# The opening of a diffusion block: modulation weights re-laid, and two steps handed to GpSimd

## The chip, the cores and the metric

One core of one Trainium2 chip. The time is device microseconds from a timed execution of the whole kernel; lower is better. TensorE (PE) multiplies matrices, VectorE (DVE) and ScalarE (ACT) work element by element, GpSimd (POOL) does so too on its own queue, SyncE (SP) issues the DMAs. Each of them works through its own queue in order.

## The reference

One layer of a hybrid backbone in float32: a half-step SwiGLU FFN, token mixing (an mLSTM beside a spatial gating MLP), a second FFN, a final norm. There are 1024 latent tokens (`x`) and 256 context tokens (`ctx`), 1024 channels, and an FFN width of 2816. What matters here is how the layer starts:

```python
mods   = split(silu(c) @ w_ada + b_ada, 9)              # nine vectors of 1024, for the latent tokens
mods_c = split(silu(c_ctx)[None] @ w_ada + b_ada, 9)    # the same for the context

def ffn_sublayer(h, shift, scale, gate, g, w_in, w_out):
    hn = rmsnorm(h, g) * (1 + scale) + shift
    a, b = split(hn @ w_in, 2)
    return h + 0.5 * gate * ((silu(a) * b) @ w_out)

h  = ffn_sublayer(x + pos_emb, mods[0],   mods[1],   mods[2],   g_ffn1, w_ffn1_in, w_ffn1_out)
hc = ffn_sublayer(ctx,         mods_c[0], mods_c[1], mods_c[2], g_ffn1, w_ffn1_in, w_ffn1_out)
...                                                     # mixing, second FFN, final norm
```

`w_ada` is 1024 x 9216, that is nine parts of 1024 columns. Its first two parts give the shift and the scale of the first FFN, and no product of that FFN can begin without them.

## The kernel before, in words

Everything is held with channels on the 128 partitions, so a tensor of 1024 channels is eight blocks `d`. Large products run in three passes: each operand is split into a rounded part and a remainder (`hi`, `lo`), and for each block the passes are hi x hi, hi x lo and lo x hi (`mm3`, L182). `split` (L145, L146) makes the two parts of a weight: ACT copies the rounded one, VectorE subtracts for the remainder.

The kernel opens with the context's first FFN product (`pa`, `pb`, 22 steps `f`), since the context is small. `W` (class `Weights`) brings its weights: `load` issues the DMA of a raw weight of 128x1024 (L126) and splits it into `hl`; up to three are held.

Ahead of the first product stand four strands of work:

- *Norm of the context* (`nct`, class `Norm`). `sq` squares a block on ACT and adds it to `acc` on the engine given to the constructor (L209, seven adds of 128x256). `rstd` sums `acc` over the partitions on PE (L214), takes the inverse root on VectorE (L758 to L770), and writes it on two diagonals (`diag`, L224, L225). `bcast` spreads it over the partitions on PE (`rb`, L230). `scaled0` multiplies the eight blocks of the context by it on VectorE (L938).
- *Shift and scale* from the first two parts of `w_ada`, cut into four column quarters `qt` and four row groups `kp`, sixteen pages of 512 KB. Each page holds for two row blocks 256 columns of part 0 and 256 of part 1. Quarters 0, 1 and 3 are multiplied on PE (`ada_rows`, L850), copied on ACT (`ada_copy`), turned on PE (`ada_flip`, L859), and finished on VectorE (`ada_done`, L879 and L887). Quarter 2 is multiplied on VectorE instead: `side(kp, ...)` does four multiply-adds of 128x512 a page (L791, L793), then `ada_red` transposes and reduces (L797, L798), and `ada_side` finishes it (L867, L871).
- *The modulated context*: `mod0(d, d+1)` makes two blocks on ACT (L931 and L932: scale and shift, rounded copy) and their remainders (L934), the even block's on POOL and the odd one's on VectorE.
- *The first weights* (`W.load`).

In this opening the order on PE, VectorE and ACT is the order in which the program writes its steps (`manual_schedule`), up to the end of the first step `f == 0`; POOL's and SyncE's are set by a scheduler. Filling matmuls (`idle`, L922, products of constants into a bank that nobody reads) keep PE at work in between. The products of step 0 start with six of the eight blocks for `pa`; `last0` (quarter 3's `ada_flip`, `ada_done`, then `mod0(6, 7)` and the third weight) is put between `pa` and `pb`.

The pages of `w_ada` are read from the tensor as it is, 8 x 128 x 9216, by `ada_page` in two DMAs each. The other seven parts are read much later by `ada_load` (L782), in pieces of 128x512, for the gates and the later sublayers.

Of the kernel before, what the change touches and what calls it, by code (L numbers as in the profile page):

```python
# [9 lines left out]
F32 = mybir.dt.float32  # L10
# [3 lines left out]
ALU = mybir.AluOpType  # L14
# [9 lines left out]
NKT = D // 128  # L24
# [31 lines left out]
def _build(ctx, tc, nc, a, out):  # L56
    V, S, G, T = nc.vector, nc.scalar, nc.gpsimd, nc.tensor
# [5 lines left out]
    hnp = pool("hn")  # L63
# [37 lines left out]
    def mm_ps(name):  # L101
        return ps.tile([128, 512], F32, name=name, tag="mm", bufs=4)
# [4 lines left out]
    class Weights:  # L107
# [7 lines left out]
            self.held = 0  # L115
            self.n = 0

        def load(self):
            n, i, w = self.order.popleft()
            src = a[n][i]  # L120
            if self.n % 4 < 2:
                raw = self.pool.tile([128, w], F32, name="raw", tag="raw", bufs=2)
            else:
                raw = hnp.tile([128, w], F32, name="raw", tag="pg0" if self.n == 2 else "pg1", bufs=8)
            self.n += 1
            nc.sync.dma_start(raw, src)  # L126
            hl = self.pool.tile([128, 2, w], F32R, name="hl", tag="hl", bufs=3)
            split(hl, raw)
            self.ready.append((n, i, hl))
            self.held += 1  # L130

# [9 lines left out]
            while self.order and self.held < 3:  # L141
                self.load()

    def split(hl, src):
        hi = S.copy(hl[:, 0, :], src)  # L145
        return hi, V.tensor_sub(hl[:, 1, :], src, hl[:, 0, :].bitcast(F32))  # L146

    def behind(fn, ins):

# [628 lines left out]

    def ada_load(page, m, hf, k):
        pgt = page()  # L780
        o = m * 1024 + hf * 512
        nc.sync.dma_start(pgt, a["w_ada"][k, :, o:o + 512])  # L782
        return pgt

# [51 lines left out]
    QW = 1024 // NQ  # L836
    QD = QW // 128
    KP = 512 // QW

    def ada_page(qt, kp, tag):  # L840
        pg = hnp.tile([128, KP, 2, QW], F32, name="adapg", tag=tag, bufs=8)
        for i in range(KP):
            src = a["w_ada"][kp * KP + i].rearrange("p (m c) -> p m c", m=9)[:, 0:2, qt * QW:(qt + 1) * QW]
            nc.sync.dma_start(pg[:, i], src)
        return [pg[:, i].rearrange("p m c -> p (m c)") for i in range(KP)]

    def ada_rows(pr, pgs, kp):
        for i, pg in enumerate(pgs):
            k = kp * KP + i
            T.matmul(pr[0:2, 0:2 * QW], sc2[:, :, k], pg, start=k == 0, stop=k == NKT - 1, skip_group_check=True)  # L850

    def ada_copy(pr):
        row = t2("adrow", shape=(2, 2 * QW))
        S.copy(row, pr[0:2, 0:2 * QW])
        return row
# [42 lines left out]
    W = Weights([("w1i", f, 1024) for f in range(2 * NF)], "w1")  # L898
    A = Stage("1", "w1i", 3)
    h = A.h  # L900
    hcp = [fxpage("hc", F32, (128, 4, 256)) for _ in range(2)]
    hc = [hcp[d // 4][:, d % 4, :] for d in range(NKT)]
# [17 lines left out]
    def idle(n):  # L920
        for _ in range(n):
            T.matmul(junk[:, 0:128], ones, ones, start=True, stop=True)  # L922

    hncp = [fxpage("hnc", F32R, (128, 2, 2, 256)) for _ in range(4)]
    hnc = [hncp[d // 2][:, d % 2] for d in range(NKT)]
    nct = Norm(hc, 256, V)

    def mod0(*ds):
        ts = [t2("nt")[:, 0:256] for _ in ds]
# [6 lines left out]
    def scaled0():  # L936
        for d in range(NKT):
            V.tensor_tensor(hc[d], hc[d], nct.rb, ALU.mult)  # L938
# [5 lines left out]
    def side(kp, pgs):  # L944
        for i, pg in enumerate(pgs):
            for q in range(2):
                ada_acc(V, sides[q], pg, q, kp * KP + i, kp + i == 0)

    load_c(hcp, 4)
    pgs = {}  # L950
    for qt, kp in ((2, 0), (0, 0), (0, 1), (2, 1), (0, 2), (0, 3), (2, 2), (1, 0), (1, 1), (2, 3), (1, 2), (1, 3),
                   (3, 0), (3, 1), (3, 2), (3, 3)):
        pgs[qt, kp] = ada_page(qt, kp, "pg1" if qt % 2 else "pg0")
    idle(30)
    for d in range(NKT):
        nct.sq(d)
    side(0, pgs[2, 0])
    prs = {0: mm_ps("adr")}
    ada_rows(prs[0], pgs[0, 0], 0)
    nct.rstd()  # L960
    ada_rows(prs[0], pgs[0, 1], 1)
    idle(3)
    side(1, pgs[2, 1])
    ada_rows(prs[0], pgs[0, 2], 2)
    nct.bcast()
    ada_rows(prs[0], pgs[0, 3], 3)
    row = ada_copy(prs[0])
    scaled0()
    side(2, pgs[2, 2])
    idle(4)  # L970
    pc = sm_ps("adc")
    ada_flip(pc, row)
    ada_done(0, pc)
    mod0(0, 1)
    prs[1] = mm_ps("adr")
    for kp in range(NKT // KP):
        ada_rows(prs[1], pgs[1, kp], kp)
    row = ada_copy(prs[1])
    side(3, pgs[2, 3])
    reds = [cp.tile([128, 32], F32, name="adred", tag="adred", bufs=2) for _ in range(2)]  # L980
    for acc, red in zip(sides, reds):
# [4 lines left out]
    ada_flip(pc, row)  # L986
    ada_done(1, pc)
    mod0(2, 3)
    ada_rows(prs[3], pgs[3, 1], 1)
    ada_side(2, reds)  # L990
    for kp in (2, 3):
        ada_rows(prs[3], pgs[3, kp], kp)
    W.load()
    mod0(4, 5)
    row = ada_copy(prs[3])
    W.load()
# [157 lines left out]
    hc = [hcp[d // 2][:, d % 2, :] for d in range(NKT)]  # L1154
# [4 lines left out]
    for f in range(NF):  # L1159
        hl, g = wready.popleft()  # L1160
# [14 lines left out]
    nct = Norm(hc, 256, V)  # L1175
# [951 lines left out]
    m = [fxpage("m", F32, (128, 1024)) for _ in range(NKT)]  # L2127
# [101 lines left out]
def layout(x, c, ctx, c_ctx, w_ada, b_ada, g_ffn1, w_ffn1_in, w_ffn1_out, g_mix, w_in, b_gates,  # L2229
           conv_qk_w, conv_qk_b, g_head, g_sgu, w_s, b_s, w_branch_a, w_branch_b, w_out,  # L2230
           g_ffn2, w_ffn2_in, w_ffn2_out, g_final):
    f = np.float32

    def A(v):
        return np.asarray(v)
    x, c, ctx, c_ctx = A(x)[0], A(c)[0], A(ctx)[0], A(c_ctx)
    win = A(w_in)[0]
    off = {}
    o = 0
    for n, w in (("q", 1024), ("k", 1024), ("v", 1024), ("g", 16), ("o", 1024), ("u", 1024), ("vs", 1024), ("ga", 1024), ("gb", 1024)):  # L2240
        off[n] = win[:, o:o + w]
        o += w
    r = {}
    r["xT"] = np.ascontiguousarray(x.T).reshape(8, 128, 1024)
    r["cT"] = np.ascontiguousarray(ctx.T).reshape(8, 128, 256)
    parts = {
        "b_ada": _cols(A(b_ada)[0]), "g_ffn1": _cols(A(g_ffn1)[0]), "g_mix": _cols(A(g_mix)[0]),
        "g_ffn2": _cols(A(g_ffn2)[0]), "g_final": _cols(A(g_final)), "g_head": _cols(A(g_head)[0]),
        "g_sgu": _cols(A(g_sgu)[0]), "c": _cols(c), "c_ctx": _cols(c_ctx),
        "conv_w": np.concatenate([_cols(A(conv_qk_w)[0, j]) for j in range(3)], axis=1),  # L2250
        "conv_b": _cols(A(conv_qk_b)[0]),
    }
    r["vec"] = np.ascontiguousarray(np.concatenate([parts[n] for n in VEC], axis=1))
    s = np.arange(128)
    cst = np.zeros((128, 5, 128), f)
    cst[s, 0, s] = 1.0
    cst[:, 1, :] = (s[:, None] % 32 == s[None, :] % 32)
    cst[s, 2, 127 - s] = 1.0
    cst[:, 3, :] = np.where(s[:, None] <= s[None, :], 0.0, -BIG)
    cst[:, 4, :] = np.where(s[:, None] >= s[None, :], 0.0, -BIG)  # L2260
    r["cst"] = cst.reshape(128, 640)
    quarter = D // 4
    freqs = np.exp(f(-np.log(10000.0)) * np.arange(quarter, dtype=f) / f(quarter)).astype(f)
    rr = np.arange(16, dtype=f)[:, None] * freqs
    cc = np.arange(64, dtype=f)[:, None] * freqs
    rt = np.concatenate([np.sin(rr), np.cos(rr)], axis=1).astype(f)
    ct = np.concatenate([np.sin(cc), np.cos(cc)], axis=1).astype(f)
    rt = rt.T.reshape(4, 128, 16).transpose(1, 0, 2).reshape(128, 64)
    ct = ct.T.reshape(4, 128, 64).transpose(1, 0, 2).reshape(128, 256)
    r["pos"] = np.ascontiguousarray(np.concatenate([rt, ct], axis=1))  # L2270
    r["b_gates"] = np.ascontiguousarray(A(b_gates)[0]).reshape(1, 16)
    r["b_s"] = np.ascontiguousarray(A(b_s)[0]).reshape(1, 512)
    r["wsT"] = np.ascontiguousarray(A(w_s)[0].transpose(2, 0, 1)).reshape(128, 512)
    r["w_ada"] = np.ascontiguousarray(A(w_ada)[0]).reshape(8, 128, 9216)
    for n, w in (("w1i", w_ffn1_in), ("w2i", w_ffn2_in)):
        t = _tiles(A(w)[0])
        r[n] = np.ascontiguousarray(np.stack([t[:NF], t[NF:]], axis=1)).reshape(2 * NF, 128, 1024)
    r["w1o"] = np.ascontiguousarray(A(w_ffn1_out)[0]).reshape(NF, 128, 1024)
    r["w2o"] = np.ascontiguousarray(A(w_ffn2_out)[0]).reshape(NF, 128, 1024)
    for n, k in (("wq", "q"), ("wk", "k"), ("wo", "o"), ("wu", "u"), ("wga", "ga"), ("wgb", "gb")):  # L2280
        r[n] = _tiles(off[k])
    for n, k in (("wv", "v"), ("wvs", "vs")):
        r[n] = np.ascontiguousarray(off[k]).reshape(8, 128, 1024)
    r["wg"] = np.ascontiguousarray(off["g"].reshape(8, 128, 16).transpose(1, 0, 2)).reshape(128, 128)
    r["w_a"] = _tiles(A(w_branch_a)[0])
    r["w_b"] = _tiles(A(w_branch_b)[0])
    r["w_o"] = _tiles(A(w_out)[0])
    return r
# [18 lines left out]
```

## Time and profile before

| | |
|---|---|
| median of 3 runs | 2649.54 us (2647.95 to 2652.47) |
| span of the profiled execution, first to last instruction | 2647.6 us |
| its own time as a run | not listed apart; the fastest run is 2647.95 us, the median 1.94 us above the span |
| TensorE matmul / weight load | 2632.7 us (99%) / 2213.3 us (84%) |
| VectorE, ScalarE, GpSimd | 1947.2 us (74%), 1202.8 us (45%), 74.2 us (3%) |
| HBM read, written | 329.11 MB, 121.32 MB, 170 GB/s over the span |

The profile shows one execution. Busy times of engines overlap. In a timeline row stand the start in us, the length in us, the engine, the line of the program, the operation, output and inputs by the program's names, and a count; an idle time ahead of the row, with what ended it, is in brackets. In the chain of waits a row is a start, a length and what the end of the kernel was waiting for then. In a row by windows stand the window and its length, the busy time of PE, PE's weight loads, VectorE, ACT and POOL, each with a count of instructions, and at the end the granted TensorE clock, the busy share of the DMA engines, and GB/s.

### The profile page before, as it was taken

Reading aid. Unit: us, or ns where it says so; the run is one execution under the profiler, and the core shown is the slowest. Engines: PE = TensorE matmul, PEld = TensorE weight load, DVE = VectorE, ACT = ScalarE, POOL = GpSimd, SP = SyncE. Lnnn points to the kernel's source line nnn. Section 1 sums busy time; section 2 is a strip of 40 time slices with the busy share of each in tenths; the row PEclk is TensorE's granted clock in tenths of the full one; section 3 lists DMA queues with packets and bytes.
Section 4 is the critical chain, followed back from the end, with each engine's and each line's share of the span. In section 5 each row is a group of like instructions: output and inputs, shape, how many; then the busy total and the mean of one; then the engine's idle time right before and its main releaser. Section 6 shows DMA issues by size and latency. Waiting matters only on the chain.

```text
span 2647.6 us, 35932 instructions
## 1 busy us (share of the span) xinstructions
PE 2632.7 (99%) x12904; PEld 2213.3 (84%) x12904; DVE 1947.2 (74%) x3490; ACT 1202.8 (45%) x2167; POOL 74.2 (3%) x158
## 2 busy tenths in 40 slices
PE   9999999999999999999999999999999999999998
PEld 6998888888889878888888888888888888888887
DVE  7988688687989646787664878777568766665855
ACT  5664444444347525564443454333256444344433
POOL 0000000000000000000000002221000000000000
PEclk9999999999999999999999999999999999999999
DMA  9833344368587122356552466547341333337654
GB/s 314 308 111 136 119 163 167 112 233 309 172 278 263 65 80 91 104 184 197 188 178 105 151 218 243 175 154 267 131 142 41 127 140 115 120 123 277 200 160 178
DMA packets 201234, 452.73 MB, mean 171 GB/s; under 512 B 20320, under 2 KB 54624, under 8 KB 201056
## 3 DMA queue, kind: packets, MB, share of 16 engines
q1 hardware_dynamic: 200624, 450.05, 49.9%
q8 instruction: 101, 1.65, 0.3%
q14 instruction: 77, 0.63, 0.1%
q10 hardware_dynamic: 432, 0.39, 0.0%
HBM read 329.11 MB, written 121.32 MB: 170 GB/s over the span
## 4 chain that ended last, share of the span: by engine, by line
PE 94%; issue 2%; DMA 2%; DVE 1%; ACT 1%; POOL 0%; SPq 0%; POOLq 0%; DVEq 0%; ACTq 0%
PE qa L411 18%; PE pq L1377 17%; PE po L535 14%; PE qb L411 14%; PE pt L1856 10%; PE pr L1296 5%; PE pa L182 2%; PE pc L1165 2%; PE pb L182 2%; PE pn L2011 2%; PE pu L1697 1%; PE pn L2009 1%; PE pkc L1356 1%; PE pvc L1453 1%; PE sp L1975 1%
## 5 line engine op out<-in xcount | busy, mean ns | idle before, releaser
L146 DVE TENSOR_TENSOR ring<-rawq,ring 128x512 fp32r<-128x512 f32 x408 | 281.0, 690 | 225.5 <-ACT ring L145 224.2
L535 PE MATMUL po<-gring,wring 128*128 128x512 f32 (+1 forms) x1896 | 423.5, 384 | 0.0
L535 PEld LDWEIGHTS po<-gring,wring 128*128 128x128 f32 x1896 | 349.6, 188 | 69.9
L145 ACT CAST ring<-rawq 128x512 fp32r<-128x512 f32 x408 | 253.4, 622 | 312.3 <-PE pq L1377 87.0
L411 PE MATMUL qa<-fc,ring 128*128 128x512 f32 x1056 | 252.4, 389 | 0.0
L411 PEld LDWEIGHTS qa<-fc,ring 128*128 128x128 f32 x1056 | 198.2, 188 | 41.5 <-DVE fc L146 0.4
L1377 PE MATMUL pq<-fc,ring 128*128 128x512 f32 x864 | 208.5, 394 | 0.0
L145 ACT CAST wring<-rw 128x512 fp32r<-128x512 f32 x154 | 95.8, 623 | 217.2 <-PE po L535 183.0
L1377 PEld LDWEIGHTS pq<-fc,ring 128*128 128x128 f32 x864 | 162.2, 189 | 33.4
L1856 PE MATMUL pt<-yp,ring 128*128 128x512 f32 x768 | 184.8, 394 | 0.0
L1856 PEld LDWEIGHTS pt<-yp,ring 128*128 128x128 f32 x768 | 143.1, 188 | 28.2
L146 DVE TENSOR_TENSOR wring<-rw,wring 128x512 fp32r<-128x512 f32 x154 | 105.6, 686 | 81.4 <-ACT wring L145 81.0
L1377 PE MATMUL pq<-fa,ring 128*128 128x512 f32 x576 | 142.4, 395 | 0.0
L1377 PE MATMUL pq<-fb,ring 128*128 128x512 f32 x576 | 138.5, 394 | 0.0
L1377 PEld LDWEIGHTS pq<-fb,ring 128*128 128x128 f32 x576 | 107.7, 188 | 23.8 <-issue 0.2
L411 PE MATMUL qa<-fa,ring 128*128 128x512 f32 x528 | 127.0, 390 | 0.0
L411 PE MATMUL qa<-fb,ring 128*128 128x512 f32 x528 | 126.5, 390 | 0.0
L411 PE MATMUL qb<-fb,ring 128*128 128x512 f32 x528 | 126.5, 389 | 0.0
L411 PE MATMUL qb<-fc,ring 128*128 128x512 f32 x528 | 126.3, 389 | 0.0
L411 PE MATMUL qb<-fa,ring 128*128 128x512 f32 x528 | 126.2, 389 | 0.0
L1377 PEld LDWEIGHTS pq<-fa,ring 128*128 128x128 f32 x576 | 106.9, 188 | 22.3 <-DVE ring L146 0.2
L793 DVE SCALAR_TENSOR_TENSOR adacc<-adapg,sc,adacc 128x512 f32<-128x512 f32 x154 | 111.7, 745 | 15.7 <-DMA adapg<-in_w_ada_dram 14.7
(366 smaller groups left out, 4643.6 us busy)
## 6 DMA issues: line engine op xcount, KB each, us to landing
adapg<-in_w_ada_dram SPq DMA_DIRECT2D x144, 256.0 KB, 3.6
fsp<-fhl SPq DMA_DIRECT2D x66, 512.0 KB, 2.7
gring<-fsp SPq DMA_DIRECT2D x66, 512.0 KB, 4.1
raw<-in_w1i_dram SPq DMA_DIRECT2D x44, 512.0 KB, 5.3
graw<-fsp SPq DMA_DIRECT2D x88, 256.0 KB, 3.6
rawq<-in_w1i_dram SPq DMA_DIRECT2D x38, 512.0 KB, 3.7
rawq<-in_w2i_dram SPq DMA_DIRECT2D x38, 512.0 KB, 3.6
fsp<-p SPq DMA_DIRECT2D x66, 256.0 KB, 2.2
```

The costliest lines, as they stand in the source:

```text
L145: hi = S.copy(hl[:, 0, :], src)
L146: return hi, V.tensor_sub(hl[:, 1, :], src, hl[:, 0, :].bitcast(F32))
L182: T.matmul(pt, x, y, start=first and i == 0, stop=i == n - 1, skip_group_check=True)
L411: T.matmul(pt, hl[:, x, sl], pages[p][k][:, y, :], start=first and i == 0, stop=i == 11, skip_group_check=not first)
L535: T.matmul(pt[:, cs], w[:, x, sl], g[:, y, cs], start=grp and kp == 0 and i == 0, stop=kp == NFP - 1 and i == 2, skip_group_check=not grp)
L793: eng.scalar_tensor_tensor(acc, pgt, sc2[:, q, k:k + 1], acc, ALU.mult, ALU.add)
L1165: T.matmul(pt, hl[d // 4][:, x, sl], g[:, y, :], start=f == 0 and d % 2 == 0 and i == 0, stop=f == NF - 1 and i == 2, skip_group_check=True)
L1296: T.matmul(self.pt[m], pg[:, x, sl], hl[:, y, :], start=first and k == 0 and i == 0, stop=k == 3 and i == 2, skip_group_check=not first)
L1356: T.matmul(self.cp[:, o:o + 256], hl[:, x, k * 128:(k + 1) * 128], hnc[kc][:, y, :], start=p == 1 and k == 0 and i == 0, stop=p in (2, 4) ...
L1377: T.matmul(pt, hl[:, x, k * 128:(k + 1) * 128], pg[k][:, y, :], start=first and k == 0 and i == 0, stop=k == 3 and i == 2, skip_group_chec ...
L1856: T.matmul(pt, hl[:, x, k * 128:(k + 1) * 128], pg[:, y, :], start=kh + k + i == 0, stop=kh == 1 and k == 3 and i == 2)
L2011: T.matmul(pn[:, 0:257], qi[:, c_, :], self.C[d][:, c_, :], start=False, stop=c_ == 1)
```

## The change

The first two parts of `w_ada` become a tensor of their own, `w_ada0`, in sixteen blocks of 128 x 1024: one page is now one contiguous block, read in one DMA with 4 KB per partition instead of two with runs of 1 KB. The rest, `w_ada`, keeps seven parts, so `ada_load` counts its columns from part 2. The pages are loaded in another order. The adds of the context's squares go from VectorE to POOL, and so does the subtraction that makes the remainder of the first weight. Of the filling matmuls 26 of the first 30 stay, and the 3 and 4 that stood later are taken out. The written order of the opening changes: quarter 0's second page comes ahead of the row sums of `rstd`; its third and fourth and quarter 1's first page come ahead of `bcast`; `side(2, ...)` moves from before quarter 0's turn to before `side(3, ...)`; two more pages of quarter 3 come ahead of `ada_side`.

```diff
-        def load(self):
+        def load(self, eng=V):
...
-            split(hl, raw)
+            split(hl, raw, eng)
...
-    def split(hl, src):
+    def split(hl, src, eng=V):
         hi = S.copy(hl[:, 0, :], src)
-        return hi, V.tensor_sub(hl[:, 1, :], src, hl[:, 0, :].bitcast(F32))
+        return hi, eng.tensor_tensor(hl[:, 1, :], src, hl[:, 0, :].bitcast(F32), ALU.subtract)
...
-        o = m * 1024 + hf * 512
+        o = (m - 2) * 1024 + hf * 512
...
     def ada_page(qt, kp, tag):
-        pg = hnp.tile([128, KP, 2, QW], F32, name="adapg", tag=tag, bufs=8)
-        for i in range(KP):
-            src = a["w_ada"][kp * KP + i].rearrange("p (m c) -> p m c", m=9)[:, 0:2, qt * QW:(qt + 1) * QW]
-            nc.sync.dma_start(pg[:, i], src)
-        return [pg[:, i].rearrange("p m c -> p (m c)") for i in range(KP)]
+        pg = hnp.tile([128, KP, 2 * QW], F32, name="adapg", tag=tag, bufs=8)
+        nc.sync.dma_start(pg.rearrange("p k c -> p (k c)"), a["w_ada0"][qt * (NKT // KP) + kp])
+        return [pg[:, i] for i in range(KP)]
...
-    nct = Norm(hc, 256, V)
+    nct = Norm(hc, 256, G)
...
-    for qt, kp in ((2, 0), (0, 0), (0, 1), (2, 1), (0, 2), (0, 3), (2, 2), (1, 0), (1, 1), (2, 3), (1, 2), (1, 3),
+    for qt, kp in ((0, 0), (0, 1), (2, 0), (0, 2), (0, 3), (2, 1), (1, 0), (1, 1), (2, 2), (1, 2), (1, 3), (2, 3),
                    (3, 0), (3, 1), (3, 2), (3, 3)):
         pgs[qt, kp] = ada_page(qt, kp, "pg1" if qt % 2 else "pg0")
-    idle(30)
+    idle(26)
     for d in range(NKT):
         nct.sq(d)
-    side(0, pgs[2, 0])
     prs = {0: mm_ps("adr")}
     ada_rows(prs[0], pgs[0, 0], 0)
+    side(0, pgs[2, 0])
+    ada_rows(prs[0], pgs[0, 1], 1)
     nct.rstd()
-    ada_rows(prs[0], pgs[0, 1], 1)
-    idle(3)
-    side(1, pgs[2, 1])
     ada_rows(prs[0], pgs[0, 2], 2)
-    nct.bcast()
     ada_rows(prs[0], pgs[0, 3], 3)
     row = ada_copy(prs[0])
+    prs[1] = mm_ps("adr")
+    ada_rows(prs[1], pgs[1, 0], 0)
+    nct.bcast()
+    side(1, pgs[2, 1])
     scaled0()
-    side(2, pgs[2, 2])
-    idle(4)
     pc = sm_ps("adc")
     ada_flip(pc, row)
     ada_done(0, pc)
     mod0(0, 1)
-    prs[1] = mm_ps("adr")
-    for kp in range(NKT // KP):
+    for kp in (1, 2, 3):
         ada_rows(prs[1], pgs[1, kp], kp)
     row = ada_copy(prs[1])
+    side(2, pgs[2, 2])
     side(3, pgs[2, 3])
...
     mod0(2, 3)
-    ada_rows(prs[3], pgs[3, 1], 1)
+    for kp in (1, 2):
+        ada_rows(prs[3], pgs[3, kp], kp)
     ada_side(2, reds)
-    for kp in (2, 3):
-        ada_rows(prs[3], pgs[3, kp], kp)
-    W.load()
+    ada_rows(prs[3], pgs[3, 3], 3)
+    W.load(G)
     mod0(4, 5)
     row = ada_copy(prs[3])
     W.load()
...
-    r["w_ada"] = np.ascontiguousarray(A(w_ada)[0]).reshape(8, 128, 9216)
+    wada = A(w_ada)[0].reshape(8, 128, 9, 1024)
+    r["w_ada"] = np.ascontiguousarray(wada[:, :, 2:]).reshape(8, 128, 7168)
+    r["w_ada0"] = np.ascontiguousarray(wada[:, :, :2].reshape(4, 2, 128, 2, 4, 256).transpose(4, 0, 2, 1, 3, 5)).reshape(16, 128, 1024)
```

## The prediction, made before the changed kernel was run

> **What bounds the kernel now.** I read the page first, then the span cut in windows, then the chain and the engines' timelines over the first 46 us, where every edit but one lies.
>
> ```profile
> span 2647.6 us, 35932 instructions
> PE 94%; issue 2%; DMA 2%; DVE 1%; ACT 1%; POOL 0%; SPq 0%; POOLq 0%; DVEq 0%; ACTq 0%
> ```
>
> The chain that ended last is 94% TensorE. The windows (busy time by engine; the last columns are granted clock, DMA share, GB/s) show where it is not:
>
> ```profile
> 0.00:37.20 37.20, 35.85 (x151) 17.29 (x151) 25.34 (x71) 14.78 (x33) 2.86 (x9) 1.00 0.99 326
> 100.00:2647.00 2547.00, 2534.30 (x12240) 2134.02 (x12240) 1869.85 (x3351) 1149.45 (x2082) 70.05 (x148) 1.00 0.49 165
> ```
>
> Behind 100 us TensorE is busy 2534.30 of 2547 us, so the body can give back 12.7 us at most, and the change touches nothing there but the address of the `w_ada` loads. In the first 37.2 us PE looks busy too, but with filling matmuls and the small `adr` products; the first large product (`pa`) starts behind them. The chain of waits, in order of time (start, length, what), tells what it waits for:
>
> ```profile
> 1.64 4.22 DMA hc<-in_cT_dram
> 5.88 0.42 ACT acc L205
> ...
> 10.16 0.87 DVE adacc L791 x2
> ...
> 26.16 2.73 DVE adacc L793 x4
> ...
> 35.91 1.24 DVE hl L146
> 37.14 0.04 issue
> 37.19 2.18 PE pa L182 x16
> ```
>
> Nearly every piece between 6.6 and 37.1 us is VectorE. So I price the change as a shift of the moment at which `pa` has its weight's remainder, 37.19 us; what comes later moves with it, since PE is full from there on. VectorE's own timeline (start, length, line, operation), which the sum is made on:
>
> ```profile
> 6.63 3.60 DVE L209 TENSOR_TENSOR acc<-acc,sq 128x256 f32<-128x256 f32 x7 [5.44 <-ACT sq L208]
> 10.16 0.87 DVE L791 TENSOR_SCALAR adacc<-adapg,sc 128x512 f32<-128x512 f32 x2
> 10.95 1.41 DVE L793 SCALAR_TENSOR_TENSOR adacc<-adapg,sc,adacc 128x512 f32<-128x512 f32 x2
> 12.27 0.15 DVE L758 TENSOR_SCALAR rs_x<-p 128x2 f32<-128x2 f32 x1
> 14.86 0.64 DVE L225 SCALAR_TENSOR_TENSOR diag<-cst,rs_y,diag 128x128 fp32r<-128x128 f32 x2 [0.47 <-ACT diag L224]
> 15.42 2.73 DVE L793 SCALAR_TENSOR_TENSOR adacc<-adapg,sc,adacc 128x512 f32<-128x512 f32 x4
> 18.07 2.73 DVE L938 TENSOR_TENSOR hc<-hc,rb 128x256 f32<-128x256 f32 x8
> 20.72 2.73 DVE L793 SCALAR_TENSOR_TENSOR adacc<-adapg,sc,adacc 128x512 f32<-128x512 f32 x4
> 30.89 0.69 DVE L798 TENSOR_REDUCE adred<-adtr 128x16 f32<-128x512 f32 x1
> 35.91 1.23 DVE L146 TENSOR_TENSOR hl<-raw,hl 128x1024 fp32r<-128x1024 f32 x1
> 37.13 0.88 DVE L934 TENSOR_TENSOR hnc<-nt,hnc 128x256 fp32r<-128x256 f32 x1
> ```
>
> **The loads.** Thirty-two DMAs of 256 KB in runs of 1 KB become sixteen of 512 KB in runs of 4 KB, in another order: `(0,0) (0,1) (2,0) ...` where `(2,0)` was first. SyncE has half the issues, which pays nothing, since it was waiting for landings anyway. Rates, from two windows, one with `w_ada` pages, one with `w1i` weights in runs of 4 KB:
>
> ```profile
> 28.00:29.00 1.00, 1.00 (x3) 0.17 (x2) 1.00 (x3) 0.51 (x1) 0.00 (x0) 1.00 1.10 348
> 33.00:34.00 1.00, 1.00 (x3) 0.17 (x2) 0.12 (x1) 0.97 (x3) 0.72 (x1) 1.00 1.08 408
> 9.73 1.88 PE L850 MATMUL adr<-adapg,sc 128*2 128x512 f32 x4
> ```
>
> At 348 GB/s a page of 524 KB takes 1.51 us, at 408 GB/s 1.28 us. The second page was there at 9.73 us (third row: its products begin), so the pages' stream starts at 9.73 - 2 x 1.51 = 6.7 us, and the new third page, `(2,0)`, lands at 6.7 + 3 x 1.28 = 10.6 us; `side(0)` on VectorE waits for it, where it began at 10.16 us before. All sixteen are in by 27.2 us instead of 30.8 us, but their readers are VectorE's chain, so that gain lies beside it. If the rate stays at 348, the page lands at 11.2 us.
>
> **Squares on POOL.** Seven adds (3.60 us) leave VectorE, but the same row-sums are still needed by `rstd`. POOL's prices (two rows with min/median/max in ns, two of its timeline), and PE's for the sums:
>
> ```profile
> L2185 POOL TENSOR_TENSOR h<-h,rbs x6: 726/730/740, 2633.5 to 2643.0; 128x256 f32<-128x256 f32 x6
> L2005 POOL TENSOR_TENSOR qi<-qT,ib x128: 447/459/958, 1583.5 to 1819.2; 128x128 f32<-128x128 f32 x128
> 32.99 0.73 POOL L934 TENSOR_TENSOR hnc<-nt,hnc 128x256 fp32r<-128x256 f32 x1 [7.34 <-ACT hnc L932]
> 36.23 1.49 POOL L934 TENSOR_TENSOR hnc<-nt,hnc 128x256 fp32r<-128x256 f32 x1 [2.52 <-ACT hnc L932]
> 11.54 0.60 PE L214 MATMUL p<-ones,acc 128*128 128x1 f32 x4
> ```
>
> An add of 128x256 is 0.73 us, so the sum, begun at 6.65 us as before, is done at 6.65 + 7 x 0.73 = 11.8 us, against 10.2 us. The 36.23 row is the warning: the same operation took 1.49 us while VectorE's `hl` subtraction (35.91 to 37.14) ran, and VectorE's next one, at 37.13, took 0.88 us, where a 128x256 one costs about 0.5 (3.60 / 7). The two engines hold each other up. `side(0)` (2.19 us from 10.16 to 12.35) now falls on the last adds: by 10.6 us POOL has done 5.4, and 1.6 x 0.73 = 1.15 us are left. One behind the other, both are done at 10.6 + 2.19 + 1.15 = 13.95 us; if nothing is held up, VectorE is free at 12.8 us; if POOL stands wholly still, the sums on PE (0.6 us) put it at 14.55 us. `rsqrt` (L758, 12.27 before) so starts 0.5, 1.7 or 2.3 us later; I take 1.7, since the 36.23 and 37.13 rows show both sides stretched.
>
> **The moved steps.** PE, which works in order, now runs two pages' products ahead of the sums and three more pages ahead of `bcast`:
>
> ```profile
> 32.88 3.60 PE L850 MATMUL adr<-adapg,sc 128*2 128x512 f32 x8
> 16.56 0.50 PE L230 MATMUL rb<-diag,onesr 128*128 128x256 f32 x2
> 36.40 0.51 PE L182 MATMUL pa<-hnc,hl 128*128 128x256 f32 x2
> 31.88 0.60 ACT L931 ACTIVATE nt<-hc,mods,smod 128x256 f32<-128x256 f32 x1 [3.37 <-DVE smod L887]
> 33.76 1.04 ACT L145 CAST hl<-raw 128x1024 fp32r<-128x1024 f32 x1
> ```
>
> The sums, 0.6 us from about 13.3 us, hide behind `side(0)`. Then three pages of 1.8 us (3.60 for two) and `bcast` end at 13.9 + 5.4 + 0.5 = 19.8 us. VectorE gets there at the same time: 3.15 us from L758 to the start of `side(1)` (12.27 to 15.42) and its 2.73 us, so 13.95 + 3.15 + 2.73 = 19.8 us. I count zero; a slower page makes it 0.5. `side(2)` moved behind `ada_done(0)` and `mod0(0, 1)` brings these forward by 2.73 us but leaves VectorE's total up to the reductions as it was: they end at 31.58 + 1.7 = 33.3 us. `side(3)`'s and qt 3's products stay behind earlier data (PE has 1.8 us a page from 20.8 us on), and the third page ahead of `ada_side` is done before the reductions; no cost.
>
> **The first weight's remainder on POOL.** ACT's copy comes 1.88 us after the first scale, as before (31.88 to 33.76), so at 35.5 to 36.5 us; the raw weight, last on SyncE behind the pages, comes earlier than before and waits for ACT. Before, VectorE had the remainder at 37.14, 2.34 us after the copy. On POOL, by the two sizes above, (730 - 447) / 128 = 2.2 ns an element, so 730 + 768 x 2.2 = 2.43 us for 128x1024. An estimate; its ends are VectorE's 1.23 us and four contended quarters, 5.96 us. VectorE has only `ada_side`'s small pieces in that stretch, so the uncontended rows decide; the upper end would make the whole 5.4 us, 2654.9 us, inside the range. 36.5 + 0.05 + 2.43 + 0.05 = 39.05 us for `pa`, 0.15 us more than the shift. `mod0(4)`'s subtraction now queues behind it on POOL, until 39.8 us; PE needs it after four of `pa`'s eight blocks, 1.45 us in, at 40.5 us: no cost. The second weight's split is unchanged and VectorE is free for it.
>
> **Filling matmuls.** Four of the thirty and the later seven leave PE's order; they are not on the chain. They cover the granted clock, 1.00 in every window above; what it costs if it falls is a rival. Sum: 1.7 + 0.15 = about 1.9 us later. The profiled span, 2647.6, would be 2649.5 us; the median of the runs shown lies 1.9 us above the span, at 2649.54, and becomes 2651.4 us.
>
> **Rivals.**
> *No holding up.* POOL and VectorE run side by side: 0.5 + 0.15 = 0.7 us, 2650.2 us. For it: most of the 128 small ones are near their minimum; against it: the 1.49.
> *Slower beyond the bound: the adds cost 1.49 us each.* The price of the 36.23 row for all seven: the sum at 6.65 + 10.4 = 17.1, L758 at 17.7 us, 5.4 later, with 0.15 some 5.6 us: 2655.1 us. It decides from 1.45 us an add. Against it: VectorE is idle for the first five.
> *Faster: the relief counts whole.* VectorE loses 3.60 + 1.23 = 4.83 us of work, and if the sum came no later than `side(0)` needs, the chain would shorten by it: 2644.7 us. It decides where L758 starts ahead of 12.27 us, for which the third page would have to land before 10.1 us and the adds to take under 0.6 us.
> *The pages gain no rate.* At 348 GB/s the third page costs 0.65 us more: 2652.1 us. For it: the first row; against it: 408 in the other. The Trainium skill, DMA: Bandwidth & Descriptors, "Where 436 GB/s comes from", holds that about 358 GB/s of HBM binds such loads, whatever their runs; by it the result is this rival's. The trace speaks against it with the 408 GB/s.
> *PE slows without the fillers.* PE stands from about 36 to 39 us, with two products inside (36.40 row). Should the clock then be half for as long as it stood, 3 us, `pa` and `pb` lose 1.5 us: 1.9 + 1.5 = 3.4 us, 2652.9 us. No window before has a clock below 1.00. The Trainium skill, TensorE: Matmul & The Clock Gate, "The HAM clock gate", puts the fall to 4/8 behind an idle window of about 3.4 us; my longest gap is under that, and no run here shows the case.
>
> **How the numbers follow.** Forecast 0.42; no holding up 0.15; no rate 0.10; slow clock 0.10; 1.49 adds 0.12; whole relief 0.11. About 0.2%, 5.3 us, is what a measurement of this kernel can tell from none. Faster than that needs more than the whole relief: 0.06. Slower: two thirds of the 1.49 case and a tail of the clock's: 0.10. The range, 2647.5 to 2655.5, holds all cases but the relief and part of the 1.49 one, with the 2.9 us by which the runs shown go over their median.
>
> **What would show it.** Third page at 10.6 us and 400 GB/s up to 27 us; seven POOL adds, the first at 0.73 us, the last two longer; L758 near 14 us; POOL's `hl` 2.4 us long; steady `pa` near 39 us; the granted clock 1.00. Wrong if L758 comes before 12.3 us, if POOL's add is far from 0.73 us, or if the body behind 100 us changes its 12.7 us of idle PE.

## The result: 5 us slower, 4.2 of them lost in the opening

| | before | changed |
|---|---|---|
| median of 9 runs, us | 2649.53 (2647.88 to 2652.47) | 2654.59 (2653.65 to 2658.77) |
| span of the profiled execution, us | 2647.6 | 2651.9 |
| `rsqrt` on VectorE (L758) starts at, us | 12.27 | 14.36 |
| `pa` gets its weight's remainder at, us | 37.19 | 39.41 |
| products of step 1 start at (PE timeline), us | 45.32 | 49.54 |

The ratio is 1.0023, 95% interval 1.0014 to 1.0032, that is 3.7 to 8.5 us. The chain's shares by engine and two windows of the changed kernel (the first from where `pa` has its remainder to where step 1 begins, the second from 54.6 us later on, as in the kernel before):

```profile
PE 93%; DMA 2%; issue 2%; DVE 2%; ACT 1%; SPq 0%; POOL 0%; POOLq 0%; DVEq 0%; ACTq 0%
39.40:49.70 10.30, 9.64 (x60) 8.88 (x61) 6.25 (x16) 7.80 (x13) 1.46 (x2) 0.85 0.80 240
104.30:2651.30 2547.00, 2534.18 (x12240) 2133.04 (x12239) 1869.50 (x3351) 1148.18 (x2082) 70.66 (x148) 1.00 0.49 165
```

The body is the same to 0.1 us: PE busy 2534.18 of 2547 us, against 2534.30. Everything lies ahead of step 1, and one column is new there: a granted clock of 0.85. The chain of waits in the opening:

```profile
3.69 7.97 DMA adapg<-in_w_ada_dram
...
11.76 1.35 DVE adacc L791 x2
...
37.07 2.31 DVE smod L885
...
39.41 0.61 ACT nt L929
...
42.84 1.14 DVE hl L146
...
44.10 0.16 DVE mods L877
```

It starts with a DMA until 11.7 us (`side(0)` waits for its page, now third), and it has a `smod` of 2.31 us, an instruction on 128x2 elements. Behind that it runs over ACT and VectorE (`mod0(4, 5)`, the second weight's split, quarter 3's finish). In the kernel before, the chain from `pa` to step 1 is nearly all PE:

```profile
39.37 0.98 PE adc L859 x8
40.34 2.35 PE pb L182 x18
42.70 1.15 PE pa L182 x6
```

The engines' timelines of the changed kernel at those places:

```profile
11.76 1.35 DVE L791 TENSOR_SCALAR adacc<-adapg,sc 128x512 f32<-128x512 f32 x2 [10.57 <-DMA adapg<-in_w_ada_dram]
14.36 0.15 DVE L758 TENSOR_SCALAR rs_x<-p 128x2 f32<-128x2 f32 x1
33.76 0.16 DVE L885 SCALAR_TENSOR_TENSOR smod<-mods,vec 128x2 f32<-128x2 f32 x1
37.07 2.30 DVE L885 SCALAR_TENSOR_TENSOR smod<-mods,vec 128x2 f32<-128x2 f32 x1
...
7.18 5.65 POOL L209 TENSOR_TENSOR acc<-acc,sq 128x256 f32<-128x256 f32 x7 [6.21 <-ACT sq L208]
37.02 2.34 POOL L146 TENSOR_TENSOR hl<-raw,hl 128x1024 fp32r<-128x1024 f32 x1 [1.16 <-ACT hl L145]
...
39.41 3.52 PE L182 MATMUL pa<-hnc,hl 128*128 128x256 f32 x16 [1.92 <-POOL hl L146]
49.54 2.79 PE L182 MATMUL pa<-hnc,hl 128*128 128x256 f32 x22
```

The same `smod` takes 0.16 us at 33.76 and 2.30 us at 37.07, ending with POOL's subtraction of the weight at 39.36 us: VectorE was held. In the kernel before, with no POOL instruction beside it, the same instruction was as short as the first one here:

```profile
34.93 0.16 DVE L887 SCALAR_TENSOR_TENSOR smod<-mods,vec 128x2 f32<-128x2 f32 x1
```

In the changed kernel `pa`'s next 16 products take 3.52 us, where the kernel before needed 2.18. The changed kernel's clock by windows:

```profile
38.00:39.40 1.40, 0.00 (x0) 0.00 (x0) 1.38 (x1) 0.00 (x0) 1.36 (x1) 0.88 0.00 0
41.00:42.00 1.00, 1.00 (x7) 1.00 (x6) 0.42 (x1) 1.00 (x3) 0.26 (x1) 0.50 1.02 334
43.00:44.00 1.00, 1.00 (x9) 0.98 (x10) 1.00 (x1) 0.00 (x0) 0.00 (x0) 1.00 0.99 403
```

So 2.1 us were there by L758, and another 2.1 us came between 33.7 us and step 1, from two candidates: VectorE held by POOL (theory H), and the slowed PE (theory C).

### The profile page after: what moved, and what is told of

It reads as the page before. It is cut to its first block, busy times and chain, and to the rows that moved or that the text cites. A ratio compares the mean times of both kernels' runs of the same rounds, so it can differ in the third digit from the quotient of the medians.

```text
span 2651.9 us, 35870 instructions
## 1 busy us (share of the span) xinstructions
PE 2631.8 (99%) x12882; PEld 2211.5 (83%) x12882; DVE 1944.9 (73%) x3482; ACT 1201.3 (45%) x2167; POOL 81.5 (3%) x166
## 4 chain that ended last, share of the span: by engine, by line
PE 93%; DMA 2%; issue 2%; DVE 2%; ACT 1%; SPq 0%; POOL 0%; POOLq 0%; DVEq 0%; ACTq 0%
PE qa L411 18%; PE pq L1374 17%; PE po L535 14%; PE qb L411 14%; PE pt L1853 9%; PE pr L1293 5%; PE pc L1162 2%; PE pa L182 2%; PE pb L182 2%; PE pn L2008 2%; PE pu L1694 1%; PE pkc L1353 1%; PE pn L2006 1%; PE pvc L1450 1%; PE pm L1810 1%
```

## The experiments

What lies behind step 1 differs between single executions (span less the start of step 1: 2602.3 us before, 2605.7 us in e4, 2599.6 us in e9), so each run is read at the start of step 1 in PE's timeline: 45.32 us before, 49.54 us changed. The expectations count it 0.16 us later, by the chain (45.48 and 49.71).

**e1 to e3: held VectorE, slowed PE, or both.** Edits to the changed kernel:

```diff
     ada_rows(prs[3], pgs[3, 3], 3)
+    idle(11)                               # e2 and e3
-    W.load(G)                              # e1 and e3
+    W.load()
     mod0(4, 5)
```

> The changed kernel with the first weight's remainder back on VectorE, all else as changed. Theory H (held): POOL's 2.34 us subtraction held VectorE's two-column smod (L885, 2.30 us at 37.07) and with it mod0(4, 5), the second weight's split and quarter 3's finish. Then smod is back near 0.16 us, mod0(4, 5) starts on ACT near 37.3 instead of 39.41 us. The remainder is made behind ada_side, at about 38.1 to 39.3 us, so pa still starts near 39.3 us. By H alone step 1 starts near 47.6 us (49.7 in the changed kernel) and the span is about 2649.8 us. Theory C (clock): PE still stands from 36 to 39.3 us, the granted clock still falls to 0.50, pa's products still take 3.5 us, quarter 3's turn still ends near 43.9 us, step 1 starts near 49.0 us and the span is about 2651.2 us.

> The changed kernel with eleven filling matmuls (3.2 us) put behind quarter 3's last rows, where PE stands. Both theories: the granted clock stays 1.00 and pa's 16 products take 2.2 us instead of 3.5. Theory C (clock): step 1 starts 1.3 us earlier, near 48.4 us, span about 2650.6 us. Theory H (held): VectorE's smod still takes 2.3 us, the second weight's split still ends near 44.0 us and holds quarter 3's finish on VectorE, so step 1 starts no more than 0.3 us earlier, span about 2651.7 us.

> The changed kernel with both: the first weight's remainder on VectorE and eleven filling matmuls ahead of pa. If H and C each hide the other (quarter 3's finish waits for the later of the split and PE's turn), this gives more than the sum of the two alone: pa at 39.3 us, 2.2 us long, step 1 near 47.6 us, 2.1 us behind the kernel before (45.5), span about 2649.7 us. What is left, 2.1 us, is then the late rsqrt (L758 at 14.36 against 12.27 us). If it comes back to the kernel before, the late rsqrt is hidden.

In e1's trace (VectorE, PE's `pb`, clock by window, step 1):

```profile
36.57 0.16 DVE L885 SCALAR_TENSOR_TENSOR smod<-mods,vec 128x2 f32<-128x2 f32 x1
43.52 3.81 PE L182 MATMUL pb<-hnc,hl 128*128 128x256 f32 x18
42.00:44.00 2.00, 2.00 (x10) 1.98 (x11) 0.38 (x2) 0.00 (x0) 0.00 (x0) 0.50 1.03 393
49.52 2.80 PE L182 MATMUL pa<-hnc,hl 128*128 128x256 f32 x22
```

e2, the same instruction and step 1, with every window of the clock at 1.00:

```profile
36.75 2.31 DVE L885 SCALAR_TENSOR_TENSOR smod<-mods,vec 128x2 f32<-128x2 f32 x1
49.24 2.80 PE L182 MATMUL pa<-hnc,hl 128*128 128x256 f32 x22
```

And e3:

```profile
36.88 0.16 DVE L885 SCALAR_TENSOR_TENSOR smod<-mods,vec 128x2 f32<-128x2 f32 x1
47.75 2.79 PE L182 MATMUL pa<-hnc,hl 128*128 128x256 f32 x22
```

| step 1 at, us | PE slows | fillers keep PE busy |
|---|---|---|
| remainder on POOL | 49.54 (changed) | 49.24 (e2) |
| remainder on VectorE | 49.52 (e1) | 47.75 (e3) |

Taking away one cause gives 0.0 or 0.3 us, taking both gives 1.8. The third page landed at different times in these executions, so that L758 started at 14.36 (changed), 13.86 (e1), 14.03 (e2) and 14.17 us (e3). Counted from L758, step 1 comes after 35.18, 35.66, 35.21 and 33.58 us, against 33.05 in the kernel before: e2's 0.3 us is the earlier page alone, and taking both causes away gives 1.6 us. The 0.5 us that e3 keeps is an add of latent tokens (`h`, L914, 0.69 us at 42.40) that VectorE runs between the steps of quarter 3's finish; in the kernel before it runs behind them. Quarter 3's finish on VectorE waits for the later of two things, the second weight's split (late because VectorE was held) and PE's turn (late because PE was slow), and in the changed kernel these ended together, at 43.98 and 43.91 us. In e1 the split was early, but the clock stayed at 0.50 from about 39.9 to 46.7 us, twice as long as in the changed kernel (39.1 to 42.5), and ate the gain; its expectation under C was right in kind, 0.7 us too good.

**e4: squares back on VectorE** (changed kernel with `nct = Norm(hc, 256, V)`).

> The changed kernel with the squares' adds back on VectorE. Theory P (page): rsqrt starts late because page (2, 0), now third, lands at 11.66 us; then side(0) runs 11.7 to 13.9 us and L758 starts near 14.0 us, only 0.4 us earlier, span 2651.5 us. Rival S (squares): POOL's adds, 0.81 us each, and their holding of VectorE are the delay; then L758 falls to about 12.3 us, step 1 starts 2 us earlier and the span is about 2649.8 us.

```profile
11.29 0.88 DVE L791 TENSOR_SCALAR adacc<-adapg,sc 128x512 f32<-128x512 f32 x2 [0.94 <-DMA adapg<-in_w_ada_dram]
13.47 0.16 DVE L758 TENSOR_SCALAR rs_x<-p 128x2 f32<-128x2 f32 x1
```

The wait for the page stays, and L758 comes 0.9 us earlier: 0.5 because the two TENSOR_SCALAR take 0.88 us instead of 1.35, and 0.5 because the page landed that much sooner in this execution (`side(0)`, which waits for it, began at 11.76 us in the changed kernel, at 11.29 here, and at 11.26, 11.39 and 11.57 in e1, e2 and e3). Theory P holds for the larger part: 1.2 of the 2.1 us remain with no square on POOL. With `side(0)` as early but the squares on POOL, e1's L758 started at 13.86 us: the squares cost about 0.4 us there. The first products of e4 ran into a clock of 0.50 from 40.0 us on, so step 1 stood at 49.63 us all the same.

**e5 and e6: one part alone on the kernel before.** e5 puts the first weight's remainder on POOL (`W.load(G)`, with `load` and `split` as changed), e6 only the squares (`nct = Norm(hc, 256, G)`).

> The kernel before with one part of the change: the first weight's remainder on POOL. Times are the start of step 1's products (45.48 us in the kernel before), since the body behind them differs by 1 to 4 us from run to run. Theory H (held): POOL's subtraction starts near 34.9 us, VectorE's smod, due at 34.93 us, is held until about 37.2 us, mod0(4, 5) and the second weight's split come 2.2 us late, and step 1 starts near 47.4 us, though pa gets its remainder at 37.2 us as before and PE's clock stays 1.00. Rival (only the clock costs): step 1 starts near 45.5 us.

```profile
34.95 2.32 DVE L887 SCALAR_TENSOR_TENSOR smod<-mods,vec 128x2 f32<-128x2 f32 x1
37.31 1.57 PE L182 MATMUL pa<-hnc,hl 128*128 128x256 f32 x11 [0.37 <-POOL hl L146]
42.00:44.00 2.00, 1.98 (x9) 1.98 (x10) 0.55 (x4) 1.51 (x3) 0.43 (x1) 0.50 0.51 141
47.80 2.80 PE L182 MATMUL pa<-hnc,hl 128*128 128x256 f32 x22
```

`pa` starts 0.1 us late, and step 1 2.5 us late: VectorE was held by 2.16 us, and the clock, which I had thought would stay, fell too (0.50 from about 41.8 to 45.2 us). Here both causes act together, and no run takes the slow clock alone out of e5; that the late `mod0(4, 5)` and second split are enough is seen in e2, where the clock stayed at 1.00.

> The kernel before with one part of the change: the squares' adds on POOL, the page order and layout as before. Theory P (the late third page cost most): page (2, 0) is first and lands long before 10 us, side(0) runs beside the adds, the adds end near 12.3 us and L758 starts near 13.0 us, 0.7 us later than before; step 1 near 46.2 us. Rival S (the adds on POOL cost): L758 near 14.3 us as in the changed kernel, step 1 near 47.5 us. If VectorE's relief of 3.6 us counted, L758 would start near 8.7 us.

```profile
6.50 6.33 POOL L209 TENSOR_TENSOR acc<-acc,sq 128x256 f32<-128x256 f32 x7 [5.53 <-ACT sq L208]
8.35 1.64 DVE L791 TENSOR_SCALAR adacc<-adapg,sc 128x512 f32<-128x512 f32 x2 [7.15 <-ACT sq L208]
9.91 2.34 DVE L793 SCALAR_TENSOR_TENSOR adacc<-adapg,sc,adacc 128x512 f32<-128x512 f32 x2
13.53 0.16 DVE L758 TENSOR_SCALAR rs_x<-p 128x2 f32<-128x2 f32 x1 [1.28 <-PE p L214]
46.68 2.79 PE L182 MATMUL pa<-hnc,hl 128*128 128x256 f32 x22
```

Both sides stretch: seven adds 6.33 us instead of 5.1, `side(0)`'s four steps about 3.9 us instead of 2.2. VectorE has no squares and still starts L758 1.3 us later, because the sums come from POOL and it stands 1.28 us for them. This lies between P (0.7 us) and S (2.0 us).

**e7: the layout alone**, in the old page order, on the kernel before.

> The kernel before with one part of the change: pages in one block each, in the old order. The pages end near 27 us instead of 30.5 at about 410 GB/s, and nothing of VectorE's chain waits for them: L758 at 12.3 us, step 1 at 45.5 us, within 0.3 us. Rival (the loads set the opening): step 1 up to 3 us earlier, near 42.5 us.

```profile
9.00:12.00 3.00, 3.00 (x19) 1.69 (x17) 2.69 (x7) 0.03 (x1) 0.00 (x0) 1.00 1.03 411
13.01 0.16 DVE L758 TENSOR_SCALAR rs_x<-p 128x2 f32<-128x2 f32 x1 [0.31 <-PE p L214]
46.08 2.80 PE L182 MATMUL pa<-hnc,hl 128*128 128x256 f32 x22
```

The rate is 411 GB/s where it was 348, and nothing comes of it: step 1 is 0.8 us later, not earlier. The context's first square came 0.3 us late here and the first fillers ran until 10.6 us instead of 9.6, so I count the 0.8 as no more than a late start of this one execution: counted from L758, step 1 comes after 33.07 us, as in the kernel before (33.05).

**e8: POOL's subtraction in four pieces**, on top of e2:

```diff
+        if eng is G:
+            for i in range(4):
+                cs = slice(i * 256, (i + 1) * 256)
+                lo = G.tensor_tensor(hl[:, 1, cs], src[:, cs], hl[:, 0, cs].bitcast(F32), ALU.subtract)
+            return hi, lo
```

> The changed kernel with eleven filling matmuls ahead of pa, as in e2, and with POOL's subtraction of the first weight cut into four of 128x256 (0.73 us each). In e2 VectorE's smod was held 2.31 us and step 1 started at 49.24 us. Theory H per instruction (VectorE waits for the POOL instruction in flight): smod is held one piece at most, under 0.9 us, mod0(4, 5) starts on ACT near 37.5 us, the second weight's split ends near 42 us and step 1 starts near 48 us. Rival (VectorE waits until POOL's queue is empty, or POOL always goes first): smod is held 2.3 to 3 us and step 1 stays at 49.2 us or later.

```profile
36.53 2.81 POOL L149 TENSOR_TENSOR hl<-raw,hl 128x256 fp32r<-128x256 f32 x4 [1.16 <-ACT hl L145]
36.58 0.69 DVE L890 SCALAR_TENSOR_TENSOR smod<-mods,vec 128x2 f32<-128x2 f32 x1
38.01 0.65 DVE L890 SCALAR_TENSOR_TENSOR smod<-mods,vec 128x2 f32<-128x2 f32 x1
47.46 2.80 PE L187 MATMUL pa<-hnc,hl 128*128 128x256 f32 x22
```

The subtraction takes 0.5 us more in all, and `smod` is held 0.69 us, by one piece, instead of 2.31. Step 1 comes 1.8 us earlier than in e2 (1.6 counted from L758, which started at 13.85 us), with the remainder still on POOL. VectorE waited for the POOL instruction in flight, no longer.

**e9: the fillers alone out of the kernel before.**

> The kernel before with one part of the change: 26 of the first 30 filling matmuls, and the 3 and 4 later ones gone. If the fillers only pass time, PE waits instead, the granted clock stays 1.00 and step 1 starts at 45.5 us, within 0.3. If they held the clock, it falls to 0.50 between 14 and 25 us and the row products (1.80 us a page) take up to twice as long; rb or the later products come late and step 1 starts 1 to 3 us later.

```profile
45.42 2.80 PE L182 MATMUL pa<-hnc,hl 128*128 128x256 f32 x22
```

Step 1 started at 45.42 us, as before, and no window of the opening had a clock under 1.00: these fillers only passed time.

**e10: a faster opening.** On the kernel before, without the 3 and 4 later fillers, `mod0` is cut in two (`mod0a` on ACT, `mod0b` the remainders), and VectorE works on while ACT does its part:

```diff
-    mod0(0, 1)
+    m01 = mod0a(0, 1)
...
     side(3, pgs[2, 3])
+    mod0b(m01)
...
-    mod0(2, 3)
+    m23 = mod0a(2, 3)
...
     ada_side(2, reds)
+    mod0b(m23)
```

> A version of the kernel before, meant to be faster than both: each of mod0(0, 1) and mod0(2, 3) is cut into its ACT part and its remainders, and VectorE's remainder is written behind side(3) or behind ada_side, so VectorE doesn't stand for ACT (1.8 us twice in the kernel before); the 3 and 4 later fillers are out. VectorE's reductions then end near 29.8 us (31.6 before) and the first weight's remainder near 34.9 us (37.1); PE's rows end near 35.2 us, pa starts near 35.3 us (37.2), step 1 near 43.6 us (45.5): about 2 us less, 2647.5 us against 2649.5 us, ratio 0.9993. If PE stands long enough ahead of pa for the granted clock to fall, that is lost again and step 1 starts at 45 us or later.

```profile
33.91 1.05 ACT L145 CAST hl<-raw 128x1024 fp32r<-128x1024 f32 x1 [1.17 <-DMA raw<-in_w1i_dram]
32.42 3.60 PE L850 MATMUL adr<-adapg,sc 128*2 128x512 f32 x8
35.95 2.48 PE L182 MATMUL pa<-hnc,hl 128*128 128x256 f32 x18
44.50 2.79 PE L182 MATMUL pa<-hnc,hl 128*128 128x256 f32 x22
```

Step 1 starts 0.8 us earlier, not 2: the raw weight's landing and PE's own row products, which end at 36 us, are next in line. Timed against the kernel before it is 2647.32 us to 2648.33, ratio 0.9996, 95% interval 0.9987 to 1.0005: not to be told from no change, though it does beat the changed kernel.

## Why the prediction was right or wrong, point by point

- *The place and the sign.* Right: the opening alone moves, later, by VectorE's chain, and the body stays. The time lies inside the range; the forecast of a change too small to measure did not hold. I summed 1.9 us, the opening lost 4.2. The path failed here: "what comes later moves with it, since PE is full from there on". The remainder reached `pa` 2.2 us late, near the forecast, but step 1 came 4.2 us late, because what lies between them waited for the held VectorE and for a PE at half its clock. The other 0.8 us between the medians' difference (5.1) and the opening's is within what single executions differ by.
- *The loads.* 410 GB/s as taken, but the third page was there at 11.7 us, not 10.6. That step failed: I let pages land one after the other at the stream's rate. A window of the changed kernel up to that landing (its last column is GB/s):

```profile
0.00:11.70 11.70, 10.41 (x58) 8.28 (x59) 0.23 (x1) 6.15 (x15) 4.57 (x12) 1.00 0.82 288
```

  That is 11.7 x 288, 3.4 MB moved, where the constants, the context and three pages are 2.85 MB: the fourth page was nearly in. Why blocks of 512 KB overlap so was not tried, and no run changes the order of the pages alone. The rival without a gain in rate is out, with 410 GB/s from 12 to 20 us.
- *Squares on POOL.* The holding up was right in kind (1.35 us where 0.87 stood). L758 came at 14.36 us against 13.95, and that it came so near is luck: the page was 1.1 us later than counted, and holding up cost about 0.4 us (e1 against e4), not the 1.15 that I had summed.
- *The moved steps.* No cost up to the reductions, as counted: L758's 2.09 us appear unchanged at the end of the reductions (33.66 against 31.58 us). What they did to PE ahead of `pa` I had not counted; it stands in the last point.
- *The remainder on POOL.* 2.34 us against 2.43, `pa` at 39.41 against 39.05 us. The step that failed stands in one sentence: "VectorE has only `ada_side`'s small pieces in that stretch, so the uncontended rows decide". I asked how VectorE would stretch POOL's instruction and not how POOL would hold VectorE's, though the 0.88 us row showed it. One held piece of 128x2 cost 2.14 us, and `mod0(4, 5)` sat behind it, and with it the second weight's split, which I had called unchanged: it began at 42.84 us instead of 38.55. The Trainium skill, GPSIMD Engine Reference, "Key points", says that GpSimd contends with VectorE instructions that have two SBUF inputs or run in a 2-port mode; the trace agrees, and the size here was the rest of the instruction in flight.
- *Slow PE, a rival at 0.10.* It came true beside the forecast, and near the size given: `pa` lost 1.3 us (1.5 priced), though beside the held VectorE step 1 lost nothing more by it (e2). The fillers taken out did not do it alone (e9), and PE kept busy ahead of `pa` does away with it (e2). PE's stand ahead of `pa` does not hang on POOL: in e1, with the remainder on VectorE, PE stands nearly as long (1.84 us against 1.92) and slows too. PE had run dry: it did quarter 3's second and third page at 28.04 us, where the kernel before did two pages from 32.88 to 36.48 us, right ahead of `pa`; only the fourth was left, at 34.04 us. The changed kernel, then e1:

```profile
28.04 3.60 PE L848 MATMUL adr<-adapg,sc 128*2 128x512 f32 x8
38.83 2.96 PE L182 MATMUL pa<-hnc,hl 128*128 128x256 f32 x16 [1.84 <-DVE hl L146]
```

  From 31.6 us to `pa` at 39.4 us PE stood for 4.7 us in four pieces. How much of this comes from the moved pages and how much from VectorE's late chain, no run separates.

## What to carry to other kernels

Before a long elementwise step goes to GpSimd, list what VectorE issues while it runs: the smallest instruction there can be held for the whole of it, and what hangs on that is the price; cutting the step in pieces bounds it. Moving work off the busiest engine gains nothing where that engine still waits for the result from a slower one. Where two late strands meet, take both away in one run before calling either harmless: here each alone gave at most 0.3 us, and both 1.8.

## What the runs showed of the hardware that I had not expected

- A VectorE instruction waited for the GpSimd instruction in flight, and no longer: a `smod` of 0.16 us took 2.30 to 2.32 us beside a POOL subtraction of 128x1024 (changed kernel, e2, e5) and 0.65 to 0.69 us beside one of 128x256 (e8).
- Windows of 0.2 us put the clock at 0.50 for 3.4 us (changed kernel, e5) or 6.8 us (e1, e4), once or twice the same length. The Trainium skill, TensorE: Matmul & The Clock Gate, "The HAM clock gate", has a free-running window of about 3.4 us, with which these lengths agree; but it lets the clock fall behind an idle window of that length, and here the longest stand on the timeline near the fall was 1.92 us (changed kernel), and in e5 0.37 us. What exactly makes it fall stays open.
